# Three orders moved in a two-layer hybrid attention kernel: weight splits, a projection's first tile, layer 1's last key stores and a row of maxima

## The chip, the cores and the metric

The kernel runs on one core of a Trainium2 chip. The metric is the device time of one execution in microseconds (us), and the median of several executions is given. The engines are TensorE (PE), VectorE (DVE), ScalarE (ACT), GpSimd (POOL) and SyncE (SP); SP and POOL issue most of the DMAs, ACT some.

## The reference

Two layers over 2048 latent tokens with a prefix of 256 context tokens, width 1024, all in float32. Layer 0 (even) runs latent attention and a gated linear attention side by side, layer 1 (odd) a two-dimensional neighbourhood attention, in which each token also sees the context.

```python
def even_mixer(h, hc, ...):
    lat = split_cols(jnp.dot(h, w_in), EVEN_SPLITS)
    cp = split_cols(jnp.dot(hc, w_in), EVEN_SPLITS)
    q_x, k_x, v_x = mla_heads(lat[0], lat[1], lat[2], *mla_p, rope)
    ...
    a_x = block_attention(q_x, concat([k_x, k_c]), concat([v_x, v_c]), scale)
    b_x, b_c = gla_bidirectional(...)
    def readout(a, b, za, zb):
        a = a * silu(za)
        b = rms_norm(b, gla_gain) * silu(zb)
        return jnp.dot(jnp.concatenate([a, b], axis=-1), w_out)
...
def neighborhood_attention(q, k, v, k_ctx, v_ctx, rpb):   # one_row
    s_lat = einsum('bqhd,brkhd->bhqrk', qr, kb) * scale + bias
    s_lat = where(col_mask, s_lat, -inf)
    s_ctx = einsum('bqhd,bchd->bhqc', qr, k_ctx) * scale
    p = softmax(concat([s_lat, s_ctx]))
...
for i in range(DEPTH):
    h = rms_norm(x, norm_g[i]) * (1 + scale) + shift
    x = x + gate * y
```

## The kernel before

The work is cut into 18 tiles of 128 tokens (NT = 18, of which NCT = 2 are context). Every large product is done in three passes over a weight and an activation that are each split into a high and a low part (`hi`, `lo`; mm3 at L120 to L122 and its stepped form at L129 to L131). A split is one ACT copy and one DVE subtraction (L380 to L383 for weights: load `wraw`, make `..h`, then `..l`). The softmaxes subtract maxima that earlier stages compute: "mx" products of keys `mk` and queries `mq` or `mz`, reduced by DVE, transposed by PE, and stored as a row of negated maxima by POOL.

In time order the stages are: the latents of layer 0 (even_latent, to about 550 us), its other products with the maxima (even_rest, to 1100), its attention woven with the gated linear attention (to 1975), the projection (project, to 2200), layer 1's queries and keys (odd_qk, to 2625), its values and gates woven with the maxima (odd_vz, to 3100), and its attention with the output (to 3671).

Which instruction stands where on each engine is set by the framework's scheduler, from the order in which the code is written, from data and buffers, and from edges that the code adds: `issue_after(x)` puts what is written under it behind the instruction x. Each engine then runs its own rows strictly in order. Buffers come from named pools; a tile with `bufs=1` is written again only when its last reader is done, a store included.

The places around the change:

- even_latent: `first` (L560 to L568) computes products of the last two tiles that belong to even_rest, in the two PSUM banks of "gm", evicts each by ACT into an SBUF tile "vn" (one buffer) and stores it from ACT's queue into `Un`. `up` uses the same "vn" for the values, stored to `Vn`. `fin` transposes qn and kn on PE and evicts them as "qkhl", whose stores go to `QT` and `KT`. even_rest puts the splits of its first two weights ("WU" and "wr1") on the list `self.ahead`.
- even_mix: the attention's steps run as a generator; at its step 18 the first two tiles of the projection's input (`pr`, `px`) are loaded. `project` then splits each tile into "prh" and "prl" and runs its 48 matmuls into "pj".
- odd_qk: keys are gathered in "okt" parts of four row tiles, and store_k writes them to `K1t` from POOL's queue, four stores of 512 KB for each of two column halves j (2 and 3). The last cells are the values of tiles 16 and 17, product j = 4 ("onat"), which store_v stores to `V1`, from POOL's queue too.
- odd_vz, maxes: for each of 16 heads a table `mtab` is loaded and masked by POOL in two operations (L1247, L1248), 16 steps R compute products and their maxima, and then the row follows: reduction "mc" on DVE (L1280), transposition on PE (L1282), negation "mr" on ACT, four stores to `M1` on POOL (L1286).

Of the kernel before, what the change touches and what calls it, by code (L numbers as in the profile page):

```python
# [17 lines left out]
P = 128  # L18
# [70 lines left out]
class Kern:  # L89
# [43 lines left out]
    def weave(self, main, side, ratio, lag, head=0):  # L133

        due, done, over = -float(head * ratio), [], 0.0
        while True:
            with ExitStack() as es:  # L140
                n = len(done) - lag - 1 + int(over)
                if n >= 0:
                    es.enter_context(self.tc.issue_after(done[min(n, len(done) - 1)].ins))
                if next(main, self) is self:
                    break
            self.pump()
            due += ratio
            while due >= 1:
                due -= 1
                r = next(side, None)  # L150
                if r is None:
                    over += 1
                else:
                    done.append(r)
        for _ in side:
            pass

    def pump(self):
# [234 lines left out]
    def even_latent(self, ws, wrest, kept):  # L393
# [5 lines left out]
        with ExitStack() as es:  # L399
# [87 lines left out]
            def up(t):  # L487
# [13 lines left out]
                kn = self.tl(sp, [P, A_HEADS, A_QK], "kn")  # L501
                vn = self.tl(sp, [P, 8, 64], "vn", bufs=1)
                sk = self.tl(sp, [P, 2, 8], "sqk")
# [57 lines left out]
            def first(t, j):  # L561
# [288 lines left out]

    def even_attention(self, ap, pp):
        nc = self.nc
# [71 lines left out]
        for j in range(4):  # L924
# [12 lines left out]
            for nb, (q0, w, kts) in enumerate(blocks):  # L937
# [18 lines left out]
                for n, kt in enumerate(kts):  # L956
# [3 lines left out]
                    for i in range(2):  # L960
# [30 lines left out]
    def even_mix(self, e1, win, hT):  # L991
# [3 lines left out]
        with ExitStack() as es:  # L995
            with ExitStack() as esa:
# [5 lines left out]
                with ExitStack() as esg:  # L1002
                    gp = self.pool(esg, "glC", side="right", reuse_waits="tile")
                    gs = self.pool(esg, "glS", bufs=2, side="right", reuse_waits="tile")
                    att = self.even_attention(ap, pp)
                    next(att)
                    self.gla(gp, gs, g1, gd, pp, "gl")
# [70 lines left out]
    def project(self, RT, tiles, xsrc, dst, w, sp, pp, ld, pre, gate, ahead):  # L1078

        for t in tiles:  # L1080
            hi, lo = [self.tl(sp, [P, KD, P], "pr" + c, F32R)[:] for c in "hl"]
            r, x = pre.pop(t) if t in pre else self.project_load(RT, t, xsrc, ld)
            self.project_split(r[:], hi, lo)
            for _ in self.project_steps(hi, lo, x, gate[1 if t < NCT else 0], w, lambda: self.tl(pp, [P, 512], "pj", bufs=4),
# [14 lines left out]
    def odd_qk(self, ws, win, hT):  # L1099
# [6 lines left out]
        with ExitStack() as es:  # L1106
# [5 lines left out]
            self.ahead += [self.od_steps(win, 0, ws), self.od_steps(win, 1, ws)]  # L1112
            pend, kt = [], {}

            def cell(t, j):
# [24 lines left out]
            def fin(t, j, n):  # L1140
# [29 lines left out]
                if r0 == 6:  # L1170
                    store_k(kt.pop(j), j0, CTX + g * 512, 512)

# [19 lines left out]
    def store_v(self, t, f, v):  # L1192
# [5 lines left out]
        for r in range(2):  # L1198
            self.nc.gpsimd.dma_start(self.V1[f].rearrange("(q a) d -> a q d", a=8)[a + r, g * 64 : g * 64 + 64, :], v[r * 64 : r * 64 + 64])

    def odd_vz(self, ws, win, hT):
# [4 lines left out]
        with ExitStack() as es:  # L1206
# [28 lines left out]
            for i in range(2):  # L1235
                for z in zq[i]:
                    nc.vector.memset(z[64 - i * 64 : 128 - i * 64].bitcast(F32), 0.0)

            def maxes():
                for h in range(16):  # L1240
# [11 lines left out]
                    for R in range(16):  # L1252
# [19 lines left out]
                        for ro, ri, rn in pieces("q", 0, g, r0, nr):  # L1272
                            for co, ci, cn in pieces("q", 1, c, c0, w):
# [6 lines left out]
                    nc.vector.tensor_reduce(out=mc[:], in_=m[:], axis=AX.X, op=ALU.max)  # L1280
                    pt = self.tl(pp, [P, 512], "mx", bufs=5)
                    nc.tensor.transpose(pt[:16, :P], mc[:], self.ident[:])  # L1282
                    r = self.tl(mp, [P, P], "mr", F32R, bufs=1)
                    self.act(r[:16], pt[:16, :P], AF.Copy, scale=-1.0)
                    for g in range(4):
                        nc.gpsimd.dma_start(self.M1[h, g * 512 : g * 512 + 512].rearrange("(a c b) -> c a b", a=8, c=4),  # L1286
                                            r[4 * g : 4 * g + 4].rearrange("c (a b) -> c a b", a=8).bitcast(F32))

# [419 lines left out]
```

## Time and profile before

| what | us |
|---|---|
| median of 3 runs (lowest to highest) | 3676.13 (3675.64 to 3685.73) |
| the profiled execution | 3673.37 |
| its span in the trace | 3671.6 |
| mean granted clock of TensorE | 0.987 |
| PE idle in the stretch 2620 to 2640 | 9.0 |
| PE idle in the stretch 1975 to 1985 | 4.9 |
| PE idle in the stretch 530 to 540 | 6.0 |

In a row of a timeline stand the start, the duration, the engine, the line of the program, the operation, out<-in with the program's tile names, and in brackets how long the engine was idle before it and what ended that. A row of waits gives the waiting group, what it waited for, the total, the count and the longest. A row of a stretch gives the busy time of each engine with the number of instructions, then the clock that TensorE was granted (1.00 is full speed), the share of time that the DMA engines were busy, and GB/s. Stretches are in us from the start of the span. Line numbers are those of the kernel before; after the change they are 8 to 40 higher.

### The profile page before, as it was taken

What the parts mean: (1) busy time and instruction counts of PE and PEld (TensorE: products, weight loads), DVE (VectorE), ACT (ScalarE), POOL (GpSimd) and SP (SyncE); (2) the same over time, 40 slices, a digit from 0 to 9 for tenths busy, and PEclk for the clock granted to TensorE, in tenths of its full rate; (3) what the DMA queues carried; (4) which work ended last, traced back from release to release, by engine and by line L of the source; (5) the groups of instructions that cost most, each with busy time, mean ns of one, the idle gap of its engine ahead of it and who ended that gap; (6) DMA issues with size and microseconds to landing.
All of it is one profiled execution on the core that took longest, in us unless ns stands there. A gap on an engine that the chain in (4) does not pass through costs nothing.

```text
span 3671.6 us, 51764 instructions
## 1 busy us (share of the span) xinstructions
PE 3558.3 (97%) x18404; PEld 2746.8 (75%) x18404; DVE 2360.8 (64%) x4846; ACT 1438.0 (39%) x2740; POOL 1239.9 (34%) x1376
## 2 busy tenths in 40 slices
PE   7999989999999999999999999999899999999899
PEld 6988988888886666655656887888788887656577
DVE  4677666888876676687765335455578784666733
ACT  5545541111115555555654114444422222555510
POOL 1434330101011121221311224333334342888863
PEclk9999999999999999999999999999999999999999
DMA  7455453222243142243623544555734446888672
GB/s 260 139 155 159 132 171 110 86 74 84 69 116 88 54 126 63 89 121 91 185 71 118 166 142 134 155 156 154 234 126 139 133 125 181 211 220 220 187 236 100
DMA packets 365780, 512.25 MB, mean 140 GB/s; under 512 B 26081, under 2 KB 245297, under 8 KB 359618
## 3 DMA queue, kind: packets, MB, share of 16 engines
q1 hardware_dynamic: 320754, 417.69, 38.7%
q0 software_dynamic: 22112, 63.26, 5.6%
q10 hardware_dynamic: 22656, 27.99, 2.2%
q8 instruction: 146, 2.39, 0.3%
q14 instruction: 112, 0.92, 0.1%
HBM read 329.45 MB, written 179.37 MB: 139 GB/s over the span
## 4 chain that ended last, share of the span: by engine, by line
PE 79%; DVE 6%; issue 5%; DMA 5%; POOL 3%; ACT 2%; SPq 0%; DVEq 0%; ACTq 0%; POOLq 0%
PE gm L129 9%; PE gm L130 9%; PE gm L131 9%; PE av L905 5%; PE mx L651 4%; PE st L963 3%; PE st L964 3%; PE st L965 3%; PE st L1361 2%; PE o L1395 2%; PE pj L129 2%; PE pj L131 2%; PE pj L130 2%; PE st L129 2%; PE st L131 2%
## 5 line engine op out<-in xcount | busy, mean ns | idle before, releaser
L954 DVE TENSOR_TENSOR acc<-acc,apt 128x512 f32<-128x512 f32 x512 | 365.6, 738 | 150.7 <-ACT apt L106 147.8
L106 ACT ACTIVATE apt<-st 128x512 f32<-128x512 f32 (+1 forms) x592 | 344.6, 594 | 281.0 <-PE st L965 245.8
L652 DVE TENSOR_REDUCE mm<-mx 128x1 f32<-128x512 f32 (+1 forms) x656 | 389.3, 629 | 82.0 <-PE mx L651 75.1
L905 PE MATMUL av<-apt,av 128*64 128x512 f32 (+1 forms) x1184 | 286.4, 597 | 0.0
L963 PE MATMUL st<-aq,akh 97*128 97x512 f32 (+1 forms) x592 | 253.0, 427 | 4.6 <-ACT apt L106 2.7
L651 PE MATMUL mx<-mk,mq 96*128 96x512 f32 (+1 forms) x656 | 236.8, 373 | 5.8 <-DMA mq<-QT 3.6
L1401 POOL TENSOR_TENSOR oacc<-oacc,opt 128x576 f32<-128x576 f32 (+5 forms) x192 | 223.8, 1191 | 39.5 <-ACT rl L106 16.6
L1519 DVE TENSOR_TENSOR opt<-st,tab 128x64 f32<-128x64 f32 (+10 forms) x576 | 144.2, 317 | 140.6 <-PE st L1362 68.1
L964 PE MATMUL st<-aq,akh 96*128 96x512 f32 (+1 forms) x592 | 233.9, 395 | 0.0
L965 PE MATMUL st<-aq,akl 96*128 96x512 f32 (+1 forms) x592 | 232.8, 394 | 0.0
L1275 DVE CUSTOM_DVE_ANT_1 mx<-mx,mtab 128x225 f32<-128x225 f32 (+13 forms) x576 | 183.7, 339 | 57.6 <-PE mx L1269 42.3
L106 ACT ACTIVATE u<-gm 128x352 f32<-128x352 f32 (+1 forms) x140 | 68.6, 498 | 371.9 <-PE gm L131 208.7
L905 PEld LDWEIGHTS av<-apt,av 128*64 128x64 f32 x1184 | 81.6, 137 | 155.5 <-issue 154.1
L963 PEld LDWEIGHTS st<-aq,akh 97*128 97x128 f32 x592 | 111.8, 189 | 97.5 <-issue 43.7
L106 ACT ACTIVATE opt<-opt 128x930 f32<-128x930 f32 (+7 forms) x129 | 104.2, 810 | 110.7 <-DVE opt L1519 102.4
L651 PEld LDWEIGHTS mx<-mk,mq 96*128 96x128 f32 x656 | 121.6, 189 | 17.3 <-issue 4.0
L965 PEld LDWEIGHTS st<-aq,akl 96*128 96x128 f32 x592 | 112.8, 191 | 25.2
L964 PEld LDWEIGHTS st<-aq,akh 96*128 96x128 f32 x592 | 113.4, 192 | 17.8
L129 PE MATMUL gm<-w1h,hhi 128*128 128x512 f32 x288 | 117.3, 407 | 7.7 <-ACT onat L106 7.7
L106 ACT ACTIVATE x<-px,modB,modA 128x128 f32<-128x128 f32 x272 | 99.3, 469 | 56.8 <-PE px L331 53.9
L129 PE MATMUL gm<-w0h,hhi 128*128 128x512 f32 x288 | 115.9, 402 | 1.9 <-DVE hhi L343 1.9
L130 PE MATMUL gm<-w1l,hhi 128*128 128x512 f32 x288 | 115.6, 401 | 0.0
(479 smaller groups left out, 9895.0 us busy)
## 6 DMA issues: line engine op xcount, KB each, us to landing
q<-Q SPq DMA_DIRECT2D x48, 512.0 KB
H<-x ACTq DMA_DIRECT2D x36, 512.0 KB
adaw<-ada_w SPq DMA_DIRECT2D x64, 256.0 KB
x<-H SPq DMA_DIRECT2D x32, 512.0 KB
wraw<-w_od SPq DMA_DIRECT2D x64, 256.0 KB
K1t<-okt POOLq DMA_DIRECT2D x32, 512.0 KB, 7.5
kt<-K1t SPq DMA_DIRECT2D x32, 512.0 KB
mtab<-rpb_q SPq DMA_DIRECT2D x16, 899.0 KB
```

What stands on the lines that cost most here:

```text
L106: return self.nc.scalar.activation(out, in_, func, **kw)
L129: self.nc.tensor.matmul(out, lh(k), rh(k), start=j == 0, stop=False)
L130: self.nc.tensor.matmul(out, lh(k), rl(k), start=False, stop=False)
L131: yield self.nc.tensor.matmul(out, ll(k), rh(k), start=False, stop=j == n - 1)
L651: mm = nc.tensor.matmul(ps[:, :w], q[:A_QK, (t % 6) * P : (t % 6) * P + P], k[:A_QK, k0 : k0 + w], start=True, stop=True)
L652: nc.vector.tensor_reduce(out=m[:, t, n : n + 1], in_=ps[:, :w], axis=AX.X, op=ALU.max)
L905: nc.tensor.matmul(O[j, nb][i * 64 : i * 64 + 64, :w], V[j, kt // TT][:, kt % TT, i * 64 : i * 64 + 64], pts[i][:, :w], start=n == 0, stop ...
L954: nc.vector.tensor_tensor(out=acc[i][:, :w], in0=a[:, :w], in1=pts[i][:, :w], op=ALU.add)
L963: nc.tensor.matmul(ps[:, :w], kh[: A_QK + 1, i, kq], qh[: A_QK + 1, :w], start=True, stop=False)
L964: nc.tensor.matmul(ps[:, :w], kh[:A_QK, i, kq], ql[:A_QK, :w], start=False, stop=False)
L965: mm = nc.tensor.matmul(ps[:, :w], kl[:A_QK, i, kq], qh[:A_QK, :w], start=False, stop=True)
L1401: self.psum = nc.gpsimd.tensor_tensor(out=a, in0=a, in1=pts[:, :, a0 - r0 : a1 - r0, :], op=ALU.add)
```

## The change

Four edits. All instructions stay, in the same number.

1. even_rest's "WU" splits are wrapped in `held`, which puts each of their steps behind `self.evicted`, the ACT eviction of the last `first`; "vn" gets two buffers.
2. Only tile 0 of the projection is loaded ahead, and its split is made inside the attention, at head pair 3, block 4, key tile 9. Its high part takes a tile "prh", its low part the second buffer of "px". Tile 1 is loaded and split as all others are.
3. In odd_qk the last store_k of each half (g = 3) is put off, behind the value store of tile 16.
4. In odd_vz the row of maxima of head h is made behind step R = 5 of head h + 1 (the last head's at the end).

```diff
+    def held(self, steps):
+        while True:
+            with self.tc.issue_after(self.evicted.ins):
+                if next(steps, self) is self:
+                    return
+            yield
...
-                vn = self.tl(sp, [P, 8, 64], "vn", bufs=1)
+                vn = self.tl(sp, [P, 8, 64], "vn", bufs=2)
...
-                u = self.tl(sp, [P, LAT_CHUNK], "vn", bufs=1)
-                self.act(u[:], ps[:])
+                u = self.tl(sp, [P, LAT_CHUNK], "vn", bufs=2)
+                self.evicted = self.act(u[:], ps[:])
...
-            self.ahead += [self.rest_steps(win, 0, ws, "WU"), self.rest_steps(win, 1, wp, "wr1")]
+            self.ahead += [self.held(self.rest_steps(win, 0, ws, "WU")), self.rest_steps(win, 1, wp, "wr1")]
...
                     add(n, pts)
+                    if (j, nb, n) == (3, 4, NT // 2):
+                        ahead()
...
+                    def split():
+                        r = pre[0][2]
+                        hi, lo = self.tl(ld, [P, KD, P], "prh", F32R, bufs=1), self.tl(ld, [P, KD, P], "px", F32R)
+                        self.project_split(r[:], hi[:], lo[:])
+                        pre[0] = (hi, lo, *pre[0][2:])
...
-                        pre = {t: self.project_load(self.RT, t, self.i["xin"], ld) for t in range(2)}
+                        pre[0] = (None, None, *self.project_load(self.RT, 0, self.i["xin"], ld))
...
                     self.store_v(t, 0, n)
+                    while last:
+                        with self.tc.issue_after(self.vstore.ins):
+                            store_k(*last.pop())
...
-                    store_k(kt.pop(j), j0, CTX + g * 512, 512)
+                    last.append((kt.pop(j), j0, CTX + g * 512, 512))
+                    if g < 3:
+                        store_k(*last.pop())
...
+            def row(h, mc):
+                pt = self.tl(pp, [P, 512], "mx", bufs=5)
+                nc.tensor.transpose(pt[:16, :P], mc[:], self.ident[:])
+                r = self.tl(mp, [P, P], "mr", F32R, bufs=1)
+                self.act(r[:16], pt[:16, :P], AF.Copy, scale=-1.0)
+                for g in range(4):
+                    nc.gpsimd.dma_start(self.M1[h, g * 512 : g * 512 + 512].rearrange("(a c b) -> c a b", a=8, c=4),
+                                        r[4 * g : 4 * g + 4].rearrange("c (a b) -> c a b", a=8).bitcast(F32))
...
                         yield mm
+                        if R == 5 and h:
+                            row(*turn)
                     mc = self.tl(mp, [P, 16], "mc", bufs=1)
                     nc.vector.tensor_reduce(out=mc[:], in_=m[:], axis=AX.X, op=ALU.max)
...
+                    turn = (h, mc)
+                row(*turn)
```

How the rows move at three places, first on ACT at the end of the latents (qkhl, kn, sql: tiles of the last row tile; vn: evictions of `first`; WUh: the weight splits). Before:

```order
L106 ACTIVATE kn_5378<-up_5421 128x4x64
L106 ACTIVATE kn_5378<-up_5430 128x4x64
L106 ACTIVATE WUh_5694<-wraw_5732 128x1024
L106 ACTIVATE sql_5456<-kn_5378 128x512
L106 ACTIVATE WUh_5694<-wraw_5748 128x1024
L106 ACTIVATE qkhl_5564<-tp_5559,qkg_312 96x4x128
L106 ACTIVATE qkhl_5573<-tp_5568,qkg_312 96x4x128
L106 ACTIVATE vn_5510<-gm_5485 128x352
L568 DMA Un<-vn_5510 128x352
L106 ACTIVATE vn_5538<-gm_5513 128x352
```

The same place on ACT after the change:

```order
L106 ACTIVATE kn_5378<-up_5421 128x4x64
L106 ACTIVATE vn_5510<-gm_5485 128x352
L576 DMA Un<-vn_5510 128x352
L106 ACTIVATE kn_5378<-up_5430 128x4x64
L106 ACTIVATE sql_5456<-kn_5378 128x512
L106 ACTIVATE qkhl_5564<-tp_5559,qkg_312 96x4x128
L106 ACTIVATE vn_5538<-gm_5513 128x352
...
L106 ACTIVATE vn_5630<-gm_5605 128x352
L106 ACTIVATE WUh_5694<-wraw_5696 128x1024
L106 ACTIVATE WUh_5694<-wraw_5712 128x1024
L106 ACTIVATE qkhl_5638<-tp_5633,qkg_312 96x4x128
```

The first eviction vn stood behind two kn and the last two weight splits, and now stands behind one kn; all four splits now stand behind the fourth eviction, in pairs ahead of the last qkhl. On SP the stores of qkhl_5546 to qkhl_5573 stood behind the loads wraw_5732 and wraw_5748, and now stand ahead of them.

Second, on POOL at the end of odd_qk (okt: the key parts; onat and ovz: values; mtab: the first table of maxes). Before:

```order
L1177 DMA K1t<-okt_4541_22240 64x4x512 x2
L1177 DMA K1t<-okt_4542_22241 64x4x512 x2
L200 TENSOR_SCALAR oss_22822<-oss_22822 128x8
L202 TENSOR_TENSOR oss_22822<-oss_22822,mhalf_65 128x8
L1177 DMA K1t<-okt_4549_22287 64x4x512 x2
L200 TENSOR_SCALAR oss_22887<-oss_22887 128x8
L1177 DMA K1t<-okt_4550_22288 64x4x512 x2
...
L1199 DMA V<-onat_23069 64x512 x2
L1199 DMA V<-onat_23125 64x512 x2
L1199 DMA V<-ovz_23214 64x512 x2
```

The same place on POOL after the change:

```order
L1227 DMA V<-onat_23061 64x512 x2
L1205 DMA K1t<-okt_4549_22287 64x4x512 x2
L1205 DMA K1t<-okt_4550_22288 64x4x512 x2
L1205 DMA K1t<-okt_4541_22240 64x4x512 x2
L1205 DMA K1t<-okt_4542_22241 64x4x512 x2
L1227 DMA V<-onat_23125 64x512 x2
L1227 DMA V<-ovz_23214 64x512 x2
L1227 DMA V<-ovz_23277 64x512 x2
L1284 TENSOR_TENSOR mtab_23159<-mtab_23159,maskq_23140 128x1798
```

The eight stores to K1t stood ahead of both value stores of odd_qk, and now stand between those of tile 16 and those of tile 17.

Third, on POOL in the maxima (M<-mr: the four stores of one head's row; mtab: the tables of heads 2 and 3). Before:

```order
L1286 DMA M<-mr_23387 4x8x16 x4
L1247 TENSOR_TENSOR mtab_23660<-mtab_23660,maskq_23140 128x1798
L1199 DMA V<-ovz_23715 64x512 x2
L1248 TENSOR_TENSOR mtab_23660<-mtab_23660,maskq_23140 128x1798
L1286 DMA M<-mr_23652 4x8x16 x4
L1199 DMA V<-ovz_23936 64x512 x2
L1247 TENSOR_TENSOR mtab_23907<-mtab_23907,maskq_23140 128x1798
L1248 TENSOR_TENSOR mtab_23907<-mtab_23907,maskq_23140 128x1798
```

The same place on POOL after the change:

```order
L1284 TENSOR_TENSOR mtab_23652<-mtab_23652,maskq_23140 128x1798
L1227 DMA V<-ovz_23707 64x512 x2
L1285 TENSOR_TENSOR mtab_23652<-mtab_23652,maskq_23140 128x1798
L1273 DMA M<-mr_23501 4x8x16 x4
L1227 DMA V<-ovz_23928 64x512 x2
L1284 TENSOR_TENSOR mtab_23899<-mtab_23899,maskq_23140 128x1798
L1273 DMA M<-mr_23743 4x8x16 x4
L1285 TENSOR_TENSOR mtab_23899<-mtab_23899,maskq_23140 128x1798
```

The row of head 0 stood ahead of the masks of head 2's table, and now stands behind them; that of head 1 now stands between the two masks of head 3's table.

More of the change, by code (lines that the diff above doesn't have):

```diff
@@ L849, in finish, with even_attention @@
         return rc
-    def even_attention(self, ap, pp):
+    def even_attention(self, ap, pp, ahead):
         nc = self.nc
@@ L1004, in even_mix @@
                     gs = self.pool(esg, "glS", bufs=2, side="right", reuse_waits="tile")
-                    att = self.even_attention(ap, pp)
+                    pre = {}
+                    def split():
[3 more added lines that the diff above has]
+                        pre[0] = (hi, lo, *pre[0][2:])
+                    att = self.even_attention(ap, pp, split)
                     next(att)
@@ L1080, in project @@
         for t in tiles:
-            hi, lo = [self.tl(sp, [P, KD, P], "pr" + c, F32R)[:] for c in "hl"]
-            r, x = pre.pop(t) if t in pre else self.project_load(RT, t, xsrc, ld)
-            self.project_split(r[:], hi, lo)
+            if t in pre:
+                hi, lo, r, x = pre.pop(t)
+            else:
+                hi, lo = [self.tl(sp, [P, KD, P], "pr" + c, F32R)[:] for c in "hl"]
+                r, x = self.project_load(RT, t, xsrc, ld)
+                self.project_split(r[:], hi, lo)
             for _ in self.project_steps(hi, lo, x, gate[1 if t < NCT else 0], w, lambda: self.tl(pp, [P, 512], "pj", bufs=4),
@@ L1112, in odd_qk @@
             self.ahead += [self.od_steps(win, 0, ws), self.od_steps(win, 1, ws)]
-            pend, kt = [], {}
+            pend, kt, last = [], {}, []
             def cell(t, j):
@@ L1198, in store_v @@
         for r in range(2):
-            self.nc.gpsimd.dma_start(self.V1[f].rearrange("(q a) d -> a q d", a=8)[a + r, g * 64 : g * 64 + 64, :], v[r * 64 : r * 64 + 64])
+            self.vstore = self.nc.gpsimd.dma_start(self.V1[f].rearrange("(q a) d -> a q d", a=8)[a + r, g * 64 : g * 64 + 64, :], v[r * 64 : r * 64 + 64])
     def odd_vz(self, ws, win, hT):
@@ L1278, in maxes @@
                         yield mm
+                        if R == 5 and h:
+                            row(*turn)
                     mc = self.tl(mp, [P, 16], "mc", bufs=1)
                     nc.vector.tensor_reduce(out=mc[:], in_=m[:], axis=AX.X, op=ALU.max)
[L1281 to L1287, printed above, removed]
+                    turn = (h, mc)
+                row(*turn)
             cells = self.cells(list(range(NT))[::-1], (4, 5, 6, 7), lambda t, j: (j > 4 or t < NT - 2) and (j < 6 or t >= NCT))
```

## The prediction

> **What bounds the kernel now.** I read the page first, then TensorE's waits, then the stretches around the longest of them, then the timelines of the engines that end those waits. The page's first part and its fourth (the chain that ended last):
>
> ```profile
> PE 3558.3 (97%) x18404; PEld 2746.8 (75%) x18404; DVE 2360.8 (64%) x4846; ACT 1438.0 (39%) x2740; POOL 1239.9 (34%) x1376
> ...
> PE 79%; DVE 6%; issue 5%; DMA 5%; POOL 3%; ACT 2%; SPq 0%; DVEq 0%; ACTq 0%; POOLq 0%
> ```
>
> TensorE (PE) is busy for 3558.3 of 3671.6 us, so 113 us at most can be won by waiting less; the change takes away no matmul and no other instruction. What can move is where PE stands still, and how long its clock stays low after that. Four of its waits, as total us, times, longest:
>
> ```profile
> PE gm L129 <- ACT onat L106: 7.7, 1, 7.7
> ...
> PE mx L1282 <- DVE mc L1280: 6.6, 10, 1.9
> PE gm L120 <- ACT vn L106: 6.0, 1, 6.0
> PE pj L129 <- ACT prh L106: 4.9, 2, 2.5
> ```
>
> They are 25.2 us together, and each stands at one of the four places that the diff touches. The stretches around three of them (length, then busy time of PE, PEld, DVE, ACT and POOL, granted clock, DMA share, GB/s):
>
> ```profile
> 530.00:540.00 10.00, 4.02 (x15) 3.77 (x16) 8.69 (x17) 4.39 (x6) 4.37 (x4) 0.63 0.93 271
> 540.00:550.00 10.00, 8.79 (x50) 8.39 (x49) 1.39 (x2) 2.63 (x5) 0.00 (x0) 0.86 0.38 126
> 1975.00:1985.00 10.00, 5.10 (x15) 3.42 (x13) 4.53 (x5) 3.23 (x4) 1.26 (x1) 0.74 0.37 104
> 2620.00:2630.00 10.00, 3.46 (x17) 2.27 (x15) 5.58 (x9) 5.43 (x9) 1.14 (x2) 0.92 0.78 247
> 2630.00:2640.00 10.00, 7.54 (x20) 5.93 (x21) 5.12 (x10) 4.16 (x7) 1.04 (x2) 0.57 0.81 249
> ```
>
> Each long wait is paid for twice: once as idle time, and once as a clock of 0.57 to 0.86 when the matmuls resume. Everywhere else PE is nearly full, so time won at these places isn't hidden by something longer; it is lost again only where what comes next isn't ready.
>
> **Part A, the end of the latents (held splits, two buffers for vn).** ACT's timeline, then two rows of PE's:
>
> ```profile
> 528.11 0.64 ACT L106 ACTIVATE kn<-up 128x256 f32<-128x256 f32 x2
> ...
> 536.11 0.46 ACT L106 ACTIVATE vn<-gm 128x352 f32<-128x352 f32 x1
> ...
> 542.54 0.47 ACT L106 ACTIVATE vn<-gm 128x352 f32<-128x352 f32 x1 [5.97 <-DMA Un<-vn]
> ```
> ```profile
> 536.62 0.66 PE L120 MATMUL gm<-W1h,hhi 128*128 128x352 f32 x1 [5.97 <-ACT vn L106]
> ```
> ```profile
> 565.60 0.36 PE L651 MATMUL mx<-mk,mq 96*128 96x256 f32 x1 [3.61 <-DMA mq<-QT]
> ```
>
> The eviction at 536.11 stands on ACT behind two weight splits and four other rows that the order of before shows; PE waits 5.97 us for it, and the next eviction waits as long for the one buffer to be stored. The order of after puts this eviction right behind the first kn, at some 528.5, and all four splits behind the last eviction, and the next eviction has a second buffer. So PE's 5.97 us go. The low clock behind them goes as well: (1 - 0.63) x 4.02 + (1 - 0.86) x 8.79 = 2.7 us of the two stretches. The stores of qkhl then stand on SP ahead of the held weight loads, and PE's first maxima, which need the keys and queries from there, lose most of their 3.61 us; I count 3.0. What is added: the held splits come two at a time in front of the last qkhl evictions, for which PE's transposes of kn wait, with ACT and DVE taking some 1.06 and 1.2 us for each split; that is about 3.7 us of new wait. Sum: -6.0 - 2.7 - 3.0 + 3.7 = **-8 us**. Ends: -12 if the new wait falls away, -3 if the 3.61 us stay and the new wait is 6.
>
> **Part B, the start of the project stage (tile 0 split within the attention).** One row of ACT, and the stretch that the split moves into:
>
> ```profile
> 1980.46 1.06 ACT L106 ACTIVATE prh<-pr 128x1024 fp32r<-128x1024 f32 x1 [2.66 <-POOL rc L847]
> ```
> ```profile
> 1865.00:1975.00 110.00, 110.00 (x463) 61.24 (x462) 62.40 (x93) 55.04 (x94) 3.29 (x2) 1.00 0.14 39
> ```
>
> PE loses the two waits for prh, 4.9 us, and (1 - 0.74) x 5.10 = 1.3 us of clock in 1975 to 1985; the clock is not yet full in the stretch behind that, for which I add 0.8. After, tile 0's split (one ACT copy of 1.06 us, one DVE subtraction) runs some 75 ACT rows earlier, where ACT works 55 of 110 us and DVE 62: that cover is wide, and without it one apt would be late by 1.06 us. PE then has all of tile 0's 48 matmuls ready, some 11 us at one per 0.23, and tile 1's two loads, now issued behind the loop, and its split have that time to arrive; the DMA share there is 0.14. Sum -4.9 - 1.3 - 0.8 + 0.5 for what the scores lose = **-6.5 us**, ends -8 and -4.
>
> On the clock, the Trainium skill ("TensorE: Matmul & The Clock Gate", Part 1: The HAM clock gate) says that it drops to half after about 3.4 us without work and comes back after about 3.4 us of work. The waits here are 2.5 us at the longest, under that, and still the stretch shows 0.74: the few matmuls between them did not keep it up. By the rule taken gap by gap part B would be -4.4; I go by the row.
>
> **Part C, layer 1's last key stores.** PE, ACT, the K1t tile's own view, and the stretch in which they land:
>
> ```profile
> 2632.47 0.79 PE L129 MATMUL gm<-w1h,hhi 128*128 128x512 f32 x1 [7.72 <-ACT onat L106]
> ```
> ```profile
> 2631.30 0.63 ACT L106 ACTIVATE w2h<-wraw 128x512 fp32r<-128x512 f32 x1 [1.64 <-DMA wraw<-w_od]
> 2631.83 0.58 ACT L106 ACTIVATE onat<-gm 128x512 f32<-128x512 f32 x1
> ```
> ```profile
> L1177 POOL DMA_DIRECT2D K1t<-okt x32: 624/636/1062, 2306.8 to 2607.5; - x32
> ...
> DMA to landing us min/median/max: 2.6/6.5/12.5
> ```
> ```profile
> 2610.00:2620.00 10.00, 9.32 (x45) 7.68 (x46) 3.08 (x5) 1.70 (x3) 3.57 (x4) 1.00 1.00 297
> ```
>
> Eight stores of 512 KB, 4.2 MB, share the DMA engines with the weights w2, for which ACT's splits wait; the eviction that PE needs is behind these. At 297 GB/s the 4.2 MB are 14 us of the engines. Behind the value store they no longer stand before the weights. PE's idle time from 2620 to 2640 is 10 - 3.46 + 10 - 7.54 = 9.0 us, and its clock loses (1 - 0.92) x 3.46 + (1 - 0.57) x 7.54 = 3.5 us: **12.5 us to win at most**.
>
> The stores don't vanish, though. On SP and PE, behind them:
>
> ```profile
> 2637.96 0.33 SPq L1244 DMA_DIRECT2D mk<-K  x1
> ...
> 2649.28 0.48 SPq L1256 DMA_DIRECT2D mq<-Q  x1
> ```
> ```profile
> 2653.06 0.28 PE L1262 MATMUL mx<-mk,mz 128*128 128x256 f32 x1
> ```
>
> The loads of mk and mtab go into memory that okt and onat held, so they start only once the stores out of it have landed. That is a wait that the change adds: on SP, mk, then mtab, mq and layer 1's reloads are queued behind it; on POOL, tile 17's value stores and the masks of mtab. Before, all eight had landed by 2620 (2607.5 + 12.5), and mk went at 2637.96, behind tile 17's value stores. After, the stores start with the eviction of tile 16's values, by my estimate at 2616 to 2618, and need 14 us at the full rate, to 2632, or two times the longest landing, 25 us, for two batches of four, to 2643; then the value stores of tile 17. So mk goes between 2633 and 2645. The second mq, which needs the buffer of the first, went 11.3 us after mk; by that the first mx can run 11 us after mk, between 2644 and 2656 instead of at 2653. With the gemms alone PE would be there at 2653 - 9 = 2644. I take mk at 2638, the row of before, in the middle: mx at 2649, with PE there at 2644 and waiting some 5 us. **-4 us**; ends -12 and +4 (mx at 2656 and a low clock behind it).
>
> The Trainium skill ("DMA: Bandwidth & Descriptors", Issuing engines are not separate DMA queues) says that transfers from all issuing engines run on the same 16 DMA engines and interleave. It speaks against this part: another place in the order moves the collision from w2 to mk and mtab. The share of 1.00 above agrees; by it alone C would be nought.
>
> **Part D, the row of maxima, moved behind step 5 of the next head.** The groups of the tiles mc, mtab and mr, and the stretch:
>
> ```profile
> L1282 PE MATMUL mx<-ident,mc x16: 269/269/277, 2683.3 to 3070.5; 128*16 128x128 f32 x16
> ```
> ```profile
> L1247 POOL TENSOR_TENSOR mtab<-mtab,maskq x16: 3202/3206/3223, 2648.6 to 3019.8; 128x1798 f32<-128x1798 f32 x16
> L1248 POOL TENSOR_TENSOR mtab<-mtab,maskq x16: 3710/3726/4177, 2654.9 to 3023.1; 128x1798 f32<-128x1798 f32 x16
> ```
> ```profile
> L1286 POOL DMA_DIRECT2D M<-mr x64: 568/582/657, 2684.1 to 3073.2; - x64
> ```
> ```profile
> 2680.00:3080.00 400.00, 392.45 (x1931) 327.55 (x1930) 307.63 (x1292) 102.48 (x171) 167.83 (x152) 1.00 0.42 131
> ```
>
> The transpose runs 16 times, one head every (3070.5 - 2683.3) / 15 = 25.8 us, and waits for DVE's reduction mc in 10 of them, 6.6 us of the 7.55 us that PE idles in the stretch. Six steps later, 6/16 x 25.8 = 9.7 us, mc is long done; the last head's transpose has no next head and keeps its wait. I count **-5.5 us**; -3 if mx matmuls then wait for DVE instead, -7 at best. With the transpose go one ACT copy and four stores on POOL, 4 x 0.58 = 2.3 us.
>
> **Elsewhere** the order moves the tail of the gated linear attention (gl) by up to 68 PE rows against the attention. PE idles 765 - 756.5 = 8.5 us there:
>
> ```profile
> 1100.00:1865.00 765.00, 756.50 (x3767) 474.11 (x3766) 546.11 (x786) 427.11 (x862) 171.89 (x166) 0.99 0.35 102
> ```
>
> I give it +2, ends -3 and +4, half of what it idles now.
>
> **Sum** against the profiled execution, 3673.37 us (span 3671.6): -8 - 6.5 - 4 - 5.5 + 2 = -22, so 3651.4. The median of the runs is 2.8 above that execution; so **3654 us**.
>
> **Rivals.**
> 1. *The key stores become the bound of the first maxima.* They take 25 us, mk goes at 2645, mx at 2656, PE stands longer and restarts at a low clock: C is +4 instead of -4, 3662 us. For it: mk waits for every one of these stores. Against: by 2616 most of the weights that they shared the engines with have arrived. The rule of the page on DMA, above, is this one.
> 2. *Waits are replaced at A and in the gl tail.* The held splits cost 6 us at the transposes instead of 3.7, the 3.61 us stay, gl costs 4: A -3, gl +4, 3661 us; with a third of B lost as well, 3663.
> 3. *Slower: POOL falls behind in the maxima.* In the order of after, the four stores of row h stand before the second mask of table h + 2 and wait for step 5 of head h + 1; then 2.3 + 3.73 = 6.0 us must fit into the 10/16 x 25.8 = 16 us until that table is read. From 10 us of lateness on, each of 15 heads loses what is over: 3 us each give 45 us, 3699 us. Against: POOL works 167.83 of 400 us there.
> 4. *Little moves*: all upper ends together, C +4, A -3, B -4, D -3, gl +4: -2, 3674 us.
>
> **How the numbers follow.** Forecast 0.55 (3642 to 3661), rival 1 0.20, rival 2 0.13, rival 3 0.05, rival 4 0.07. About 0.3% (11 us) is what can be told from no change: below 3665.1 is faster, above 3687.2 slower. Faster: 0.55, 0.16 of rival 1 and 0.07 of rival 2, 0.78; slower 0.05; same 0.17. The range reaches from A -12, B -8, C -8, D -7, gl -1, which is -36 (3640), to 3669, some 7 us above rivals 1 and 2; rivals 3 and 4 and the tails stay out.
>
> **What would show it.** A: no wait of gm L120 for vn, a new one of a transpose for qkhl. B: no wait of pj near 1977. C: the w1 matmuls start near 2623 at full clock; mx at 2649, after a wait for mk or mq. D: no wait of the transposes for mc. Wrong if mk goes at 2650 or later, if mtab's masks end after the head that reads them begins, or if gl stalls the attention.

## The result and the profile after

The changed kernel takes 3656.43 us (median of 4, 3655.85 to 3659.02) against 3677.03 of the kernel before (median of 4, 3675.64 to 3685.73). The ratio is 0.9942, with a 95% interval of 0.993 to 0.9954: 17 to 26 us less. Its profiled execution has a span of 3654.3 us, 17.3 less than that of before. PE's busy time is the same, so the time came out of its waits. The page's first part:

```profile
PE 3557.3 (97%) x18404; PEld 2752.6 (75%) x18404; DVE 2352.1 (64%) x4846; ACT 1432.0 (39%) x2740; POOL 1232.1 (34%) x1376
```

PE's waits after the change, from 500 to 3090 us (total, times, longest):

```profile
PE gm L129 <- ACT onat L106: 6.9, 1, 6.9
...
PE mx L1299 <- ACT mz L106: 4.9, 1, 4.9
...
PE tp L557 <- DVE qkhl L561: 3.8, 1, 3.8
PE gm L129 <- ACT u L106: 2.7, 1, 2.7
```

Three of the four waits at which the change aims are gone: gm L120 for vn (6.0), pj for prh (4.9) and the transposes for mc (6.6). The fourth, gm L129 for onat, is 6.9 instead of 7.7 us. Two waits are new: for u at the first place, and for mz, the copy of mq, at the third. The one of the kn transposes for qkhl has grown, from 1.2 us in the profile of before (at 549.50) to 3.8. The same stretches as before the change, with those of the third place 10 us earlier, as the work is:

```profile
530.00:540.00 10.00, 8.01 (x54) 7.68 (x52) 6.51 (x15) 5.02 (x9) 3.45 (x3) 1.00 0.73 204
540.00:550.00 10.00, 8.22 (x40) 8.18 (x41) 6.08 (x7) 4.16 (x6) 0.00 (x0) 0.66 0.84 244
...
1975.00:1985.00 10.00, 10.00 (x44) 7.99 (x43) 4.53 (x5) 3.25 (x4) 1.29 (x1) 1.00 0.37 102
...
2610.00:2620.00 10.00, 2.84 (x14) 1.80 (x13) 6.23 (x10) 5.91 (x10) 4.50 (x8) 0.77 0.81 233
2620.00:2630.00 10.00, 10.00 (x33) 7.93 (x34) 0.03 (x1) 0.60 (x1) 3.55 (x7) 0.72 1.00 303
...
2640.00:2650.00 10.00, 5.12 (x24) 4.37 (x23) 1.58 (x5) 1.11 (x2) 3.25 (x2) 0.80 0.95 371
2650.00:2660.00 10.00, 10.00 (x44) 8.17 (x44) 6.05 (x34) 2.35 (x4) 9.92 (x3) 0.86 0.41 138
2680.00:3080.00 400.00, 400.00 (x1974) 335.52 (x1974) 300.96 (x1254) 104.02 (x173) 167.95 (x152) 1.00 0.46 140
```

At 1975 PE is full at full clock. From 2680 to 3080 it is full too, and does 1974 instructions where it did 1931 (not all of them the same work, since this profile is some 16 us ahead there). From 2610 to 2660 there are two stops now, and behind each the clock is low: four stretches of 0.72 to 0.86 where before had two.

To see where the 17.3 us come from, I cut every execution at the starts of the same matmuls: the last product `up` with WU, the last mx with mk and the last den of layer 0, the last pj, and the first w2 and the last mx with mk of layer 1. Stretches in us, each from one profiled execution:

| kernel | up to last mx (A) | mx to last den (attention) | den to last pj (B) | w2 to last mx (C and D) |
|---|---|---|---|---|
| before | 565.9 | 885.4 | 206.5 | 840.5 |
| full change | 559.6 | 890.4 | 198.9 | 834.7 |
| full_again, the same | 560.5 | 890.8 | 198.8 | 833.1 |
| only_held (A) | 558.6 | 891.0 | 205.9 | 838.4 |
| only_vn (half of A) | 562.5 | 887.4 | 205.7 | 841.8 |
| only_split (B) | 565.2 | 891.2 | 198.9 | 841.4 |
| only_keys (C) | 566.0 | 890.7 | 205.4 | 843.4 |
| only_row (D) | 567.8 | 888.8 | 206.9 | 836.3 |
| no_keys (A, B, D) | 560.1 | 893.6 | 198.8 | 828.7 |

A stretch that a kernel doesn't touch shows how far one execution can be trusted: 565 to 568 in the first column, 205.4 to 206.9 in the third, 838 to 842 in the fourth.

### The profile page after: what moved, and what is told of

Its sections match the earlier page's. It is cut to its first block, busy times and chain, and to the rows that moved or that the text cites. A ratio compares the mean times of both kernels' runs of the same rounds, so it can differ in the third digit from the quotient of the medians.

```text
span 3654.3 us, 51805 instructions
## 1 busy us (share of the span) xinstructions
PE 3557.3 (97%) x18404; PEld 2752.6 (75%) x18404; DVE 2352.1 (64%) x4846; ACT 1432.0 (39%) x2740; POOL 1232.1 (34%) x1376
## 5 line engine op out<-in xcount | busy, mean ns | idle before, releaser
L963 DVE TENSOR_TENSOR acc<-acc,apt 128x512 f32<-128x512 f32 x512 | 375.2, 755 | 167.1 <-ACT apt L106 164.2
L1312 DVE CUSTOM_DVE_ANT_1 mx<-mx,mtab 128x217 f32<-128x217 f32 (+12 forms) x576 | 184.2, 338 | 39.8 <-PE mx L1306 30.7
L129 PE MATMUL gm<-w1h,hhi 128*128 128x512 f32 x288 | 117.2, 407 | 6.9 <-ACT onat L106 6.9
L129 PE MATMUL gm<-w0h,hhi 128*128 128x512 f32 x288 | 114.9, 399 | 2.0 <-DVE hhi L351 1.9
L807 POOL TENSOR_TENSOR gsf<-gsf,D 64x512 f32<-64x512 f32 x17 | 25.1, 1476 | 271.1 <-DVE D L784 271.1
```

Of the source, the lines that this page charges most:

```text
L129: self.nc.tensor.matmul(out, lh(k), rh(k), start=j == 0, stop=False)
L963: nc.vector.tensor_tensor(out=acc[i][:, :w], in0=a[:, :w], in1=pts[i][:, :w], op=ALU.add)
L1312: nc.vector.tensor_tensor_reduce(out=s, in0=s, in1=tb[:, ri : ri + rn, ci : ci + cn], scale=1.0, scalar=-3e38, op0=ALU.add, op1=ALU.max, a ...
```

## The experiments

The kernels were measured on several chips, each beside the kernel before on the same chip; so ratios compare, and medians only where the chip is the same.

**Each part alone**, on the kernel before. For A, the edits of `held` and of the buffers:

```diff
-        vn = self.tl(sp, [P, 8, 64], "vn", bufs=1)
+        vn = self.tl(sp, [P, 8, 64], "vn", bufs=2)
...
-            self.ahead += [self.rest_steps(win, 0, ws, "WU"), self.rest_steps(win, 1, wp, "wr1")]
+            self.ahead += [self.held(self.rest_steps(win, 0, ws, "WU")), self.rest_steps(win, 1, wp, "wr1")]
```

> Part A alone (held splits and two buffers for vn on the kernel before). In the trace of the full change the stretch from the last up product to the last mx of layer 0 was 6.3 us shorter, and the attention behind it, whose gl tail stands 16 apt rows later in this order too, 5.0 us longer. Theory: the two belong together, so this run is 1 to 2 us under before (about 3675), with the latents' end -6 and the attention +5 in its trace. Rival: the attention's loss comes from the split that B puts into it; then the attention is unchanged here and the run is 6 us under before (about 3671).

Ratio 0.9976 (0.9966 to 0.9987), median 3668.82 against 3677.67: 5 to 12 us less. Its first stretch is 7.3 us shorter, its attention 5.6 longer than in the profile of before. The time agrees with the first stretch alone, as the rival had it, though the attention is long here too: the profile of before is the one that is short there, as the next kernels show.

For B, the split within the attention:

```diff
+                    if (j, nb, n) == (3, 4, NT // 2):
+                        ahead()
```

> Part B alone (tile 0 loaded and split within the attention on the kernel before; the gl tail stands where it stood). Theory: the two pj waits and their low clock go, -7 to -8 us, and the attention costs nothing: about 3669. Rival: the split disturbs the attention by the 5 us seen with the full change: about 3674.

Ratio 0.9983 (0.9974 to 0.9992), 3 to 10 us less; the third stretch is 7.6 us shorter, as in every kernel with B. The attention took 891.2 us, but it took 890.7 in only_keys and 888.8 in only_row, whose attention is that of before. So 885.4 is the odd one, and the split costs nothing that can be seen.

For C, the key stores put off:

```diff
-                    store_k(kt.pop(j), j0, CTX + g * 512, 512)
+                    last.append((kt.pop(j), j0, CTX + g * 512, 512))
+                    if g < 3:
+                        store_k(*last.pop())
```

> Part C alone (last key stores behind tile 16's values on the kernel before). Theory, from the trace of the full change: w1 starts 2 to 3 us earlier, but mk waits for the last of these stores and of tile 17's value stores, PE stands some 5 us before its first mx, and the part is +1 to +3 us: 3678 to 3680. Rival, the forecast: -4 us, 3673.

Ratio 1.0016 (1.0004 to 1.0028): this part makes the kernel slower, by 1 to 10 us. Its waits, from 2500 to 2700:

```profile
PE gm L129 <- ACT onat L106: 6.8, 1, 6.8
PE mx L1294 <- ACT mz L106: 5.8, 1, 5.8
```

The wait at which it aims lost 0.9 us, and one of 5.8 us is new.

For D, the row of maxima put off:

```diff
+                        if R == 5 and h:
+                            row(*turn)
```

> Part D alone (row of maxima behind step 5 of the next head on the kernel before). Theory: all 7.6 us that PE idled from 2680 to 3080 go, -7 to -8 us, about 3669; POOL keeps up. Rival: some of the waits were cover for DVE and come back at mx; -3 to -4 us, about 3673.

Ratio 0.9976 (0.9966 to 0.9985), 5 to 12 us less. In the stretch from 2680 and in the waits of 2660 to 3070 of only_row:

```profile
2680.00:3080.00 400.00, 400.00 (x1983) 335.91 (x1982) 310.91 (x1310) 105.74 (x177) 167.80 (x152) 1.00 0.44 134
```
```profile
PE tp L1250 <- DVE ovz L1247: 5.0, 1, 5.0
```

PE is full from 2680 on, and POOL's busy time is the 168 us that it was: it keeps up. But the last stretch of only_row is only 4.2 us shorter than before, since PE waits 5.0 us at 2665. DVE and POOL in only_row show what it waits for:

```profile
2654.24 10.21 DVE L391 TENSOR_TENSOR w3l<-wraw,w3h 128x512 fp32r<-128x512 f32 x1 [9.67 <-ACT w3h L106]
```
```profile
2650.21 6.39 POOL L1278 TENSOR_TENSOR mtab<-mtab,maskq 128x1798 f32<-128x1798 f32 x2
2656.55 7.33 POOL L1279 TENSOR_TENSOR mtab<-mtab,maskq 128x1798 f32<-128x1798 f32 x2
```

One subtraction of a weight split, w3l, took 10.21 us, and the row of DVE that PE needs, ovz, stands behind it. For 9.7 us of it POOL was masking the tables mtab. In the fourteen profiles, every subtraction w1l, w2l or w3l between 2400 and 2720 that overlaps one of these masks took 1.35 to 10.21 us (16 of them, in nine kernels), and every other one 0.62 to 0.73. No run moves the masks alone, so the cause is inferred from this. The full change has no such overlap: its masks start at 2646.67, after all splits of w3.

The four ratios together, -0.24 - 0.17 + 0.16 - 0.24, make -0.49%; the full change has -0.46 to -0.70%.

**The change without C**, and with half of it: first nothing put off, then only the stores of j = 3. The edits of this and the next sections are against the full change.

```diff
-                    if g < 3:
-                        store_k(*last.pop())
+                    store_k(*last.pop())
```

> The full change without part C (key stores where they stood; A, B and D stay). Theory, from the run of C alone at 1.0016: C costs, and this is 3 to 6 us faster than the full change, ratio to before about 0.993; in the trace w1 waits some 7.7 us again and the wait of the first mx of layer 1 is gone. Rival, the forecast: C is worth -4 us within the full change, ratio about 0.9955.

```diff
-                    if g < 3:
+                    if g < 3 or j != 3:
```

> The full change, but of the eight put-off key stores only the four of j = 3 are put off; the four of j = 2 go where they went before. Theory: mk waits for the last key store; with 2.1 instead of 4.2 MB behind tile 16's values that landing comes some 8 to 10 us sooner, mk 6 to 10 us sooner after w1's start, so the first mx no longer waits, while w1's wait stays near 7 us: 4 to 6 us faster than the full change. Rival: what holds mk is tile 17's value stores or the late start itself, and mk moves by less than 3 us: as the full change.

The median of no_keys is 3656.45, ratio 0.9939 (0.9927 to 0.9952). By time it can't be told from the full change (0.9942, and 0.9953 when run again); the rival's 0.9955 lies just outside its interval. Its last stretch is 828.7 us against 834.7 and 833.1 of the full change, 4 to 6 less. The DMA rows say why; SP in the full change, then POOL and the K1t tile there, then SP in half_keys and in no_keys:

```profile
2638.86 0.33 SPq L1281 DMA_DIRECT2D mk<-K  x1
```
```profile
2616.64 4.97 POOL L1205 DMA_DIRECT2D K1t<-okt  x8 [1.22 <-issue]
2621.75 0.55 POOL L1227 DMA_DIRECT2D V<-onat  x1
2624.57 0.54 POOL L1227 DMA_DIRECT2D V<-onat  x1 [2.27 <-DMA K1t<-okt]
```
```profile
DMA to landing us min/median/max: 4.6/11.2/16.0
```
```profile
2638.64 0.33 SPq L1281 DMA_DIRECT2D mk<-K  x1
```
```profile
2633.88 0.33 SPq L1280 DMA_DIRECT2D mk<-K  x1
```

w1 starts at 2619.76 in the full change, at 2628.71 in half_keys and at 2627.53 in no_keys, so mk goes 19.1, 9.9 and 6.4 us after it. Part of that is w1's own start; counted from the first w2, mk goes at 425.0, 419.5 and 413.3 us (414.0 before). In no_keys, as before, mk goes right behind the row ahead of it on SP, the load of maskq. In the full change SP stands still for 15 us ahead of mk. The last of the eight stores lands at 2637.0, and tile 17's two value stores, issued behind the eight, at 2637.3 and 2637.7, 15.6 and 13.1 us after their issue where before the longest took 5.2; mk goes at 2638.86. In the four profiles with put-off stores in which SP stands still there (the full change twice, only_keys, half_keys), mk goes 1.2 to 1.4 us after the last of tile 17's values has landed, and 1.9 to 2.8 after the last key store. So the profiles don't tell whether mk waits for the key stores themselves or for the value stores that they hold up; both come of the eight.

With four stores the first mx waits 0.3 us instead of 4.9, as the theory said. But w1 waits 8.1 us there, and half_keys, 0.995 (0.9938 to 0.9963), isn't faster than the full change by time, though I had expected 4 to 6 us; by its last stretch, 830.3, it lies between the two.

**More held at A.** In held_more the splits of WU go behind the last qkhl and those of wr1 behind the first u, without C:

```diff
-                        self.act(hi, ps[:A_QK], AF.Copy, scale=qkg[:A_QK, col : col + 1])
+                        self.evicted = self.act(hi, ps[:A_QK], AF.Copy, scale=qkg[:A_QK, col : col + 1])
...
-                    self.act(u[:, :w], ps[:, :w])
+                    self.evicted = self.act(u[:, :w], ps[:, :w])
...
-            self.ahead += [..., self.rest_steps(win, 1, wp, "wr1")]
+            self.ahead += [..., self.held(self.rest_steps(win, 1, wp, "wr1"))]
```

> no_keys, with the WU splits held behind the last qkhl eviction instead of the last vn, and the wr1 splits held behind the first u evictions. Theory: the 3.8 us wait of the kn transposes for qkhl and the 2.7 us wait for u go, W2's 48 matmuls run at full clock in about 8 us instead of 9.6, the last key stores of layer 0 and its first mx come 4 to 6 us sooner: the stretch from the last up product to the last mx of layer 0 is 3 to 6 us shorter than in no_keys. Rival: the WU splits, now later and waiting for their loads, make PE wait before the WU matmuls by as much, and the stretch is unchanged.

The fastest kernel: 3650.64 us, ratio 0.9926 (0.9912 to 0.994), against 3656.45 for no_keys on the same chip. Its first stretch is 557.3 us, 2.8 less than in no_keys, just short of the 3 to 6 expected; its waits from 520 to 600 show why:

```profile
PE mx L659 <- DMA mq<-QT: 5.6, 1, 5.6
PE gm L129 <- ACT WUh L106: 2.5, 1, 2.5
PE tp L557 <- DVE qkhl L561: 1.2, 1, 1.2
```

The wait for qkhl fell from 3.8 to 1.2 us and the one for u (0.8 in no_keys) is gone, but WU is late now by 2.5, and PE waits 5.6 us for mq, where it was 4.9. The attention is 3.0 us shorter too, 890.6 against 893.6: it differs that much between executions, and held_more also has the order of before there.

**What sets w1's wait.** In late_splits, on held_more, the splits of w2 and w3 are made behind the last onat; late_keys is the same with C; late_w3 is the full change with held_more's splits and w3 alone put behind the last onat:

```diff
-            done = lambda j: j in nxt and self.ahead.append(self.od_steps(win, nxt[j], ws))
+            done = lambda j: j in nxt and nxt[j] not in (6, 7) and self.ahead.append(self.od_steps(win, nxt[j], ws))
...
-                    self.act(n[:], ps[:].rearrange("p h d -> p (h d)"))
+                    self.evicted = self.act(n[:], ps[:].rearrange("p h d -> p (h d)"))
...
             while pend:
                 fin(*pend.pop(0))
+            self.ahead += [self.held(self.od_steps(win, j, ws)) for j in (6, 7)]
```

> held_more (no part C), with the splits of w2 and w3 made only behind the last onat eviction. Theory: what makes PE wait for w1 is ACT's order, onat behind w2 splits that wait for loads, not the key stores themselves; with onat free, the 7.5 us wait of gm L129 and the low clock behind it go, and w2's splits, 8 of some 0.65 us with their loads, are done while PE does the 48 matmuls of w1 (11 us). From the first w2 product of layer 1 to the last mx of its maxima 7 to 10 us less than in held_more, ratio to before about 0.990. Rival: w2 isn't ready when w1's matmuls end, the wait stands there instead, and 3 us or less are won.

> late_splits with part C in it (key stores behind tile 16's values). Theory: mk waits for the landing of the key stores, some 17 us after the last of them is issued, and nothing is left for them to make room for: PE waits 5 us or more for its first mx and the run is 3 to 7 us slower than late_splits. Rival: with w1 free the eight stores start some 7 us sooner, and the mx wait and its cost are gone: the same as late_splits.

> The full change with held_more's splits, and only w3's splits behind the last onat. In the order of the full change onat stands behind w3's splits where it stood behind w2's. Theory: this is why the change took only 0.9 us off the wait of gm L129; with w3 out of the way the wait falls from 6.9 to 2 us or less, w1 starts 5 to 7 us sooner, and the mx wait for mk grows by 2 to 5 us. Rival: the wait is for the loads of w2 all the same, and stays over 5 us.

PE's waits from 2560 to 2700, the first rows of late_splits, of late_keys and of late_w3:

```profile
PE gm L130 <- DVE w2l L391: 7.1, 1, 7.1
...
PE gm L129 <- ACT onat L106: 0.7, 1, 0.7
```
```profile
PE gm L129 <- ACT ovz L106: 10.1, 1, 10.1
PE gm L130 <- DVE w3l L391: 4.9, 2, 3.1
PE mx L1300 <- ACT mz L106: 3.5, 1, 3.5
```
```profile
PE gm L129 <- ACT ovz L106: 11.3, 1, 11.3
PE mx L1300 <- ACT mz L106: 2.7, 1, 2.7
...
PE gm L129 <- ACT onat L106: 0.7, 1, 0.7
```

In all three the wait for onat is 0.7 us: what held onat is ACT's order, w2's splits before the change and w3's in it. But a wait comes back within the next products. In late_keys and late_w3 it is for ovz, the eviction that now stands behind the splits. ACT in late_w3:

```profile
2630.33 1.92 ACT L106 ACTIVATE w3h<-wraw 128x512 fp32r<-128x512 f32 x3 [18.59 <-DMA wraw<-w_od]
2632.16 1.07 ACT L106 ACTIVATE ovz<-gm 128x512 f32<-128x512 f32 x2
```

ACT waits 18.59 us for weights while the eight stores move, and 17.40 in late_keys; without C, in late_splits, its longest wait for weights is 5.36. In late_splits PE waits for w2's own split. DVE and POOL there:

```profile
2641.61 8.37 DVE L391 TENSOR_TENSOR w2l<-wraw,w2h 128x512 fp32r<-128x512 f32 x2 [2.12 <-ACT w2h L106]
```
```profile
2641.57 7.25 POOL L1285 TENSOR_TENSOR mtab<-mtab,maskq 128x1798 f32<-128x1798 f32 x2
```

The first of these two subtractions took 7.77 us, and again POOL was masking mtab. So what PE waits for there is this subtraction, more than the weights.

late_splits is 0.9954 (0.9942 to 0.9967), late_w3 0.9948 (0.9934 to 0.9962): nothing won against held_more's 0.9926, and the last stretch of late_splits is 837.9 us against 826.9, 11 longer. For late_splits the rival named the place of the new wait, but not the slow subtraction. For late_w3 the theory held at w1, but it was ovz and not mx that took the wait over. late_keys is 0.9989 (0.998 to 0.9998), 3672.23 us against 3661.81 of late_splits on the same chip: C costs 10 us there, more than the 3 to 7 expected, and by another way. PE waits 3.5 us for its first mx, and mk goes right behind weight loads in which SP stood for 20.66 us; the larger wait is the 10.1 us for ovz.

**Half of A**: the two buffers without holding, on the kernel before (B, C and D are left out too).

```diff
-            self.ahead += [self.held(self.rest_steps(win, 0, ws, "WU")), ...]
+            self.ahead += [self.rest_steps(win, 0, ws, "WU"), ...]
```

> Of part A only the second buffer for vn, on the kernel before (no held splits, no B, C, D). In its order the first vn eviction already stands ahead of the last two WU splits. Theory one: the buffer does it, the 6 us wait of gm L120 goes without any holding, the stretch from the last up product to the last mx of layer 0 is 5 to 8 us shorter than before. Theory two: holding is needed, since the splits still stand ahead of the second vn and wait there for their loads (1.3 and 1.4 us before): some 2 to 3 us shorter only.

Ratio 0.9988 (0.998 to 0.9997); the first stretch is 3.4 us shorter, near the second theory. The waits from 500 to 600:

```profile
PE tp L557 <- DVE qkhl L561: 4.5, 3, 3.0
...
PE gm L120 <- ACT vn L106: 2.0, 1, 2.0
```

The second buffer takes 4 of the 6 us off this wait; holding takes the rest. The transposes of kn wait up to 3.0 us for qkhl here as well, though no split is held, so that wait is not the price of holding alone.

**The full change once more.**

> The full change once more, beside the others on one chip. Theory: ratio 0.994 again (0.993 to 0.9955), and in the trace the stretch from the last mx to the last den of layer 0, 885 us in the profile of before and 887 to 895 in all others, is over 887 again: the 5 us lost there belong to the one execution of before, not to the change. Rival: under 887, so that the gl order decides it.

Ratio 0.9953 (0.994 to 0.9967), overlapping the first. The attention took 890.8 us, as the theory said. Over all fourteen profiles, PE's order there is one of two, with the tail of gl 16 apt rows earlier (before, only_vn, only_keys, only_row, only_split, held_more and the three late kernels) or later (the other five). With the first the attention took 885.4 to 894.6 us, 889.7 in the mean; with the second 890.4 to 894.7, 892.1 in the mean. The difference of 2.4 us is smaller than the spread within one order. PE's idle time there is 8.5 to 12.6 us (10.7 in the mean) with the first and 11.7 to 14.0 (13.1) with the second, which points the same way. So a cost of some 2 us of the order is likely, but not shown by the time.

## Why the prediction came out right, point by point

3654 us was predicted and 3656.43 measured. That the sum came so near is in part luck: C was off by 8 to 10 us and D by some 4 to 6, in opposite directions. C and D together were put at -9.5, and their stretch lost 5.8 and 7.4 us in the two profiles of the full change.

**A: forecast -8, measured -6.3 in the trace** (-5 to -12 alone, by time). The wait for vn went as said; the wait for qkhl was put at 3.7 and is 3.77, but 3.2 us of such waits were there before, and that for mq fell to 1.7 (3.2 in the repeat). Not foreseen was the wait of 2.7 for u. PE's idle time in the stretch fell from 15.5 to 10.0 us, 5.5 less, where the sum had 5.3: right in total, with errors that cancel. Mis-sized was the clock: I let the 2.7 us of low clock go with the old wait, and the new wait has its own, (1 - 0.66) x 8.22 = 2.8 us in 540 to 550. What is left of the 6.3 us beside idle time is 0.8.

**B: forecast -6.5, measured -7.6.** The split is hidden. The two waits were 4.9 us, so 2.7 are left for the clock. Of these, 1.3 are in 1975 to 1985, and the stretch behind it, in the profile of before, has (1 - 0.94) x 15 = 0.9:

```profile
1985.00:2000.00 15.00, 15.00 (x63) 12.24 (x63) 6.40 (x10) 6.21 (x10) 1.29 (x1) 0.94 0.80 252
```

The Trainium skill's rule on the clock ("TensorE: Matmul & The Clock Gate", Part 1: The HAM clock gate), taken gap by gap, gave -4.4; the measurement decides for the row.

**C: forecast -4, with the ends -12 and +4; measured +1 to +10 alone, and +4 to +6 in the stretch of the full change against no_keys.** This term failed. The step at fault is "behind the value store they no longer stand before the weights", with PE at the maxima 9 us sooner. The stores did leave, but in the new order ACT makes w3's splits before onat, where it made w2's, and the sum does not have that. ACT in the full change:

```profile
2618.01 0.63 ACT L106 ACTIVATE w3h<-wraw 128x512 fp32r<-128x512 f32 x1 [0.77 <-DMA wraw<-w_od]
...
2619.12 0.59 ACT L106 ACTIVATE onat<-gm 128x512 f32<-128x512 f32 x1
```

w1 came 2.6 us sooner within its stretch and waited 6.9 us; with w3's splits moved away, in late_w3, it waited 0.7. What I had as rival 1 then took place: mk waits for landings on POOL's queue, the key stores' up to 16.0 us and tile 17's values behind them, and PE waits 4.9 us for the first mx. The price is mostly clock. From 2610 to 2630 and 2640 to 2660 it loses (1 - 0.77) x 2.84 + (1 - 0.72) x 10 + (1 - 0.80) x 5.12 + (1 - 0.86) x 10 = 5.9 us. In no_keys there is one stop, from 2620 to 2640:

```profile
2620.00:2630.00 10.00, 2.73 (x8) 1.99 (x7) 4.94 (x8) 4.72 (x8) 2.17 (x4) 0.68 0.91 274
2630.00:2640.00 10.00, 10.00 (x45) 8.18 (x44) 4.50 (x10) 3.12 (x5) 1.03 (x2) 0.97 0.83 268
```

It loses 0.9 + 0.3 = 1.2 us. The difference of 4.7 and 1.3 us more of idle time make the 6.0 us by which the last stretches of the two profiles differ. I forecast mk at 2638 and mx at 2649, and they are at 2638.86 and 2647.96. That is luck: I had put these at the times of before, while everything in front of them had moved by 10 us. Seen from the first w2, mk came 11 us later than before.

**D: forecast -5.5, measured -4 in the profile of only_row, -5 to -12 by its time, and about -9 to -12 in the other profiles with D.** The mechanism was right, the size too small: the waits of the transposes are gone. From the first to the last mx, no_keys takes 402.6 us where before takes 411.4, and the full change 400.6 where only_keys takes 409.8: 9 us each, of which 6.6 and 7.2 are idle time, and some 2 are not; the granted clock, 1.00 in either stretch from 2680, doesn't explain these. In only_row the slow subtraction beside POOL's masks takes 5.0 us of this back. Between no_keys and before, the stretch from the first w2 lost 11.8 us, with 6.6 less of idle time. Rival 3, POOL falling behind, did not come: POOL works 167.95 us as it did 167.83.

**Elsewhere: forecast +2.** The two profiles differ by 5.0 us in the attention, but so do executions with the same order; over all profiles the means of the two orders differ by 2.4, which fits the forecast without showing it.

Rival 2 came in part (the waits at A), rival 4 did not. The rule that I weighed against C (the Trainium skill, "DMA: Bandwidth & Descriptors", Issuing engines are not separate DMA queues: transfers of all engines interleave on the same 16) was nearer than my term; that C would end at nought was not borne out, since the second stop of PE costs clock.

## What to carry to other kernels

Here a load into memory that earlier stores still read, mk, went only when the stores on POOL's queue had landed, so stores that are put off put off whatever takes their buffers, or the buffers of stores queued behind them; look for that load before moving a store. A wait taken off one row of an in-order engine can show up at the next row behind the same loads or splits: with onat freed, PE waited for ovz or for w2l instead. It is worth something only where the rows behind have their inputs in time. And add up the terms in the time of the moved work, not in the times of the profile of before.

## What the runs showed that I had not expected

The attention of layer 0, with the same order on PE, took 885.4 to 894.6 us in nine executions; a difference of 5 us in one pair of profiles there shows nothing by itself. Eight stores of 512 KB issued within 5 us landed after 11.2 us in the median and 16.0 at the longest, where the same eight in two batches took 7.4 and 12.1. Taking away two waits of 2.5 us, with four matmuls between them, shortened the stretch by 7.6 us, 2.7 more than the 4.9 us of waiting. And a subtraction on DVE that takes 0.62 to 0.73 us took up to 10.21 beside POOL's masks.
